# Trunk of an encoder on one core: copies of K by block, kept convolution buffers, and other due times for decays, sweeps and first loads

## The chip, the core and the metric

The kernel runs on one core of one Trainium2 chip. The metric is the device time of one execution in microseconds (us). Of the kernel before, three runs gave a median of 2223.15 us (2220.03 to 2225.03).

The core's engines work side by side, each through its own queue in order: TensorE (PE, with its weight loads as PEld), VectorE (DVE), ScalarE (ACT), GpSimd (POOL) and SyncE (SP), which here only issues transfers. They wait for each other by semaphores.

## The reference, cut to what matters

Two groups of tokens (1024 and 256, together T = 1280, width 1024) go through two layers with shared weights and a last RMS norm. All is float32.

```python
# layer 0
proj = h @ w_in; q, k, v, g = split(proj, 4)          # 16 heads of 64
s = where(mask, (q * 64 ** -0.5) @ k.T + bias, -1e30) # windows of 8 x 16 tokens
h = x + (softmax(s) @ v * silu(g)) @ w_out
# layer 1
proj = rmsnorm(h) @ w_in                              # q, k: 8 heads of 128, v: 8 of 256, z, beta, a
qkv = silu(depthwise_conv5(proj[..., :4096], conv_w))
g = -exp(a_log) * softplus(a + dt_bias); beta = sigmoid(b)
q, k = l2norm(q) * 128 ** -0.5, l2norm(k)
o = chunked_delta(q, k, v, g, beta) + flipped(chunked_delta(flipped inputs))
h = h + (rmsnorm(o, norm_w) * silu(z)) @ w_out
```

The chunked form inverts, for each chunk of the tokens, a unit triangular matrix made of `k k^T`, beta and the decays `exp(g_i - g_j)`; then a scan over the chunks carries a state of 128 x 256 per head and direction.

## The kernel before, in words

**How order is made.** The program is traced once in Python. Long products are traced step by step, and after each matmul `side.tick(columns)` counts its columns. Side work (one attention head, one convolution, one inversion) is a generator; `side.add(chain, delay, pace)` starts it `delay` columns later, and each `yield n` in it asks for its next piece after `n * pace` more columns. So a due time is a place in the traced order, in matmul columns. A planner then orders each engine's instructions by that order and by when it holds them ready in its own model: what is ready early may move ahead. `tc.keep_in_program_order(ins)` binds an instruction behind all that was traced before it on its engine. A tile of a pool with one buffer can be taken again once the last reader of the one before has ended; a closed pool's memory is taken again in the same way.

**Layer 0.** `qk_head(h)` projects q and k of a head in three blocks of tokens (512, 512, 256), splits them into high and low parts (Q, KH, KL), and copies KH and KL from partitions 64 to 127 to partitions 0 to 63 by two transfers of all columns, behind the last block (lines 199 to 201); head 15 copies each block by itself (lines 195 to 197). `g_pair(p)` makes the gates of two heads. `attention(h)` is side work: scores S (lines 286, 287), softmax, transposes, products with V. Before the loop over heads stands `qk_head(0)`, then `g_pair(0)` alone; in the loop attention h runs beside the projections of head h + 1.

**Layer 1, projections.** `gdn_proj` goes through 32 feature blocks of w_qkv in `order` (k of a head ahead of its q and v), each of 30720 columns. A block's product goes to one of two `raw` tiles; `conv(f, r)` then runs as side work: a first tap on ScalarE into `acc`, four taps on VectorE, Silu on ScalarE, a spill to DRAM. With the k of a head, `invert` is added: the squares of k (line 649), scaling (line 657), 30 substitution steps on VectorE (lines 681, 683), called a sweep here, then after a `yield` four rounds of small products (lines 713, 720, 733, 741) with copies between them. `decays` makes the matrix E of decays for a head (product at line 606, adds on VectorE at 609, Exp on ScalarE at 615); of head 1 it is added from the first inversion. `factors` makes per-token factors for the scan from all heads' norms; it is called in the last inversion, behind its sweep. Gate products (`gate_z`) are put between.

**Layer 1, scan.** `prep(h)` loads kT, qT, vT (six pieces, by token block), E (as Al), the decay rows qe and the inverses W of a head, turns and scales them; of head 0 it runs alone beside the last gate product, of the others beside the scan of the head before. `Scan` then takes chunk pairs; its first product is line 1024. `finish` and `Out` make the gated output and the last product.

The pools: `gp` belongs to `gdn_proj` and is closed after it; `prep`, `even` and `odd` hold the scan's inputs; PSUM of the large products (`pmm`) has three buffers.

Of the kernel before, what the change touches and what calls it, by code (L numbers as in the profile page):

```python
# [8 lines left out]
F32 = mybir.dt.float32  # L9
# [3 lines left out]
OP = mybir.AluOpType  # L13
# [3 lines left out]
T = NP + NS  # L17
KD = 8
BLK = [(0, 512), (512, 512), (1024, 256)]
# [16 lines left out]
def layer0(ctx, tc, a, h1_out):  # L36
# [136 lines left out]
    with st:  # L173
# [5 lines left out]
        def qk_head(h, side=None):  # L179
            wh, wl = load_w(tc, a, a["w_qk"][h])  # L180
            Q = ap.tile([128, T], F32R, name="Q", bufs=2)
            KH = ap.tile([128, T], F32R, name="KH", bufs=2)
            KL = ap.tile([128, T], F32R, name="KL", bufs=2)
            for b, (t0, n) in enumerate(BLK):
                ps = pmm.tile([128, 512], F32, name="mm")
                proj(nc, ps[:, :n], wh, wl, XH, XL, b, side)
                c = slice(t0, t0 + n)
                t = ap.tile([128, 512], F32, name="t", bufs=2)
                nc.vector.tensor_mul(t[:, :n], ps[:, :n], rb[:, c])
                nc.scalar.activation(Q[0:64, c], t[0:64, :n], AF.Copy)  # L190
                nc.scalar.activation(KH[64:128, c], t[64:128, :n], AF.Copy, scale=0.125)
                nc.vector.tensor_sub(Q[64:128, c], t[0:64, :n], Q[0:64, c])
                nc.vector.scalar_tensor_tensor(KL[64:128, c], t[64:128, :n], 0.125, KH[64:128, c],
                                               op0=OP.mult, op1=OP.subtract)
                if h == 15:
                    for K in (KH, KL):
                        nc.scalar.dma_start(K[0:64, c].bitcast(F32), K[64:128, c].bitcast(F32))
            if h < 15:
                for K in (KH, KL):
                    nc.scalar.dma_start(K[0:64, :].bitcast(F32), K[64:128, :].bitcast(F32))  # L200
            return Q, KH, KL
# [159 lines left out]
        G, wg = {}, None  # L361
        g_pair(0, G, range(3))
        O = ap.tile([128, T], F32, name="O", bufs=1)
        GS, nV = [G, *({} for p in range(7))], V
        for h in range(16):
# [3 lines left out]
            if h < 14:  # L369
                side.add(attention(h, qkk, V, G, O), 2000, (1.6, 1.5, 1.5, 1.35)[h % 4] if h else 0.75)  # L370
            elif h == 14:
                qks, done[15] = {14: qkk}, 0
                side.add(last_pair(qks, V, G, O), 2000, 0.6)
            side.tick(0)
            q = (h + 1) // 4
            if h % 4 == 0:
# [85 lines left out]
def gdn_proj(tc, a, pmm, XH, XL):  # L462

    nc = tc.nc
    with ExitStack() as st:
# [7 lines left out]
        nc.sync.dma_start(cw, a["conv_w"])  # L473
        raw = [ap.tile([128, T + 6], F32, name=f"raw{i}", bufs=1) for i in range(2)]
        for r in raw:
# [27 lines left out]

        def conv(f, r):

            h, ch = divmod(f, 4)
            m = T + 2
            acc = ap.tile([128, T + 2], F32, name="acc")
            nc.scalar.activation(acc, r[:, 2:2 + m], AF.Copy, scale=cw[:, f, 2:3])  # L509
            yield 8000  # L510
            for i in (0, 1, 3, 4):
                tap = nc.vector.scalar_tensor_tensor(acc, r[:, i:i + m], cw[:, f, i:i + 1], acc,  # L512
                                                     op0=OP.mult, op1=OP.add)
                if i == 0:
                    tc.keep_in_program_order(tap)
            yield 14000 if ch == 1 else 20000
            th = ap.tile([128, T + 2], F32, name="th")
            tc.keep_in_program_order(nc.scalar.activation(th, acc, AF.Silu))
            nc.sync.dma_start(a["qkv_dram"][f, :, :NP], th[:, :NP])
            nc.sync.dma_start(a["qkv_dram"][f, :, NP:], th[:, NP + 2:])  # L520
            if ch == 1:
                side.add(invert(tc, a, ap, pp, h, th, D, W, WT, Z, Bs), 4000, 0.85 if h == 7 else 0.95)
# [3 lines left out]
        for h, ch in order:  # L526
# [4 lines left out]
            for b in sorted(range(3), key=lambda b: (f, b) not in a["begun"]):  # L531
# [7 lines left out]
                nc.scalar.activation(r[:, t0 + o:t0 + o + n], ps, AF.Copy)  # L539
            side.add(conv(f, r), 0)  # L540
            side.tick(0)
            if ch == 1:
                gate_blocks(1 if h in (0, 7) else 2)
        gate_blocks(1)
        side.drain()
# [91 lines left out]
def invert(tc, a, ap, pp, h, kT, D, W, WT, Z, Bs):  # L637
# [22 lines left out]
    if h == 0:  # L660
        a["side"].add(decays(tc, a, ap, pp, 1, Bs), 30000)
    sl = [slice(32 * i, 32 * i + 32) for i in range(4)]
# [45 lines left out]
    elif h:  # L708
        factors(tc, a)
    yield 42000 if h == 0 else 34000  # L710
    zt = pp.tile([128, NB, 32], F32, name="m", bufs=2)
# [46 lines left out]
def gates(tc, a, ap, pmm, pp, XH, XL):  # L758
# [5 lines left out]
    nc.gpsimd.memset(GR.bitcast(F32), 0.0)  # L764
    ab_f = ap.tile([128, T + 2], F32, name="acc")[0:64, :T]
    for b in (0, 2, 1):
# [83 lines left out]
def factors(tc, a):  # L850
# [5 lines left out]
    nc.vector.tensor_scalar(nw, nw, 0.5, None, op0=OP.mult)  # L856
    nc.vector.tensor_scalar(ss, ss, -1.0, None, op0=OP.mult)
    r = cp.tile([128, 8, NB], F32, name="r")
# [18 lines left out]


def prep(tc, a, ap, tp, p_t, h, W, X, alone=False):

# [3 lines left out]
    ident = a["ident"]  # L884
    kT = ap.tile([128, T], F32, name="kT")
    qT = tp.tile([128, T], F32, name="qT")
    nc.sync.dma_start(kT, a["qkv_dram"][4 * h + 1])
    nc.sync.dma_start(qT, a["qkv_dram"][4 * h])
    K = ap.tile([128, NB, 128], F32, name="K")
# [3 lines left out]
    sq = ap.tile([128, NB], F32, name="sq")  # L893
    vT = []

    def rows(*bs):
        for b in bs:
            t0, n = BLK[b]
            for i in range(2):
                t = tp.tile([128, n], F32, name=f"vT{b}{i}")  # L900
                nc.sync.dma_start(t, a["qkv_dram"][4 * h + 2 + i, :, t0:t0 + n])
                vT.append(t)

    if alone:
        rows(0)
    nc.sync.dma_start(AL.bitcast(F32), a["e_dram"][h])
    if alone:
        rows(1, 2)
    for d in range(2):
        nc.sync.dma_start(qe[:, d], a["eg_dram"][8 * d + h].partition_broadcast(128))  # L910
    if not alone:
        rows(0, 1, 2)
    lo, hi = slice(0, 64), slice(64, 128)
# [3 lines left out]
    X[:] = kT, V, K, qe, (AH, AL), W, sq  # L917
    yield 28000 if alone else 6000
    for c0 in range(0, NB, 4):
# [25 lines left out]
        for c1 in range(c0, c0 + n, 2):  # L945
            pv = p_t.tile([128, 2, 256], F32, name="t")
            for c in range(2):
                o = 128 * (c1 - c0 + c)
                for i in range(2):
                    nc.tensor.transpose(pv[:, c, 128 * i:128 * i + 128], vT[c0 // 2 + i][:, o:o + 128], ident)  # L950
                turned = order(nc.scalar.activation(V[:, c1 + c], pv[:, c], AF.Copy,
                                                    scale=a["nk"][:, h, c1 + c:c1 + c + 1]))
# [371 lines left out]
def trunk(ctx, tc, a):  # L1324
# [38 lines left out]
    a["ss"] = a["gc"].tile([128, 8, NB], F32, name="ss")  # L1363
    a["nrk"] = a["gc"].tile([128, 8, NB], F32, name="nrk")
    a["zp"] = left.enter_context(pool(tc, "zp", 2))
    gdn_proj(tc, a, pmm, XH, XL)
# [6 lines left out]
    side = Side()  # L1373
    side.add(prep(tc, a, ap[0], tp, p_0, 0, W[0], X[0], True), 0, 0.5)
    side.tick(0)
# [138 lines left out]
```

## Time and profile before

| What | Value |
|---|---|
| Profiled execution | 2223.32 us |
| its span, first to last instruction | 2221.5 us |
| Median of 3 runs | 2223.15 us |
| PE busy | 2151.7 us, 97% of the span |
| DVE, ACT, POOL busy | 1508.1, 1153.9, 582.8 us |
| Mean granted clock of TensorE | 0.986 |

The span is one execution, taken by the hardware profiler. "Busy" is the time in which at least one instruction of an engine runs. The granted clock is the share of TensorE's full clock; its two levels here are 0.50 (1.2 GHz) and 1.00 (2.4 GHz), and the number of a stretch is the mean. A row of waits names the engine that waited and its line, then the engine, tile and line whose end let it go; "issue" is a wait that the profile can't put down to an instruction. L713 is line 713 of the kernel before.

### The profile page before, as it was taken

How to read it: one execution, taken by the hardware profiler on the slowest of the kernel's cores; microseconds unless marked ns; L12 is line 12 of the kernel's file. 1: busy time of each engine (PE TensorE's matmuls, PEld its weight loads, DVE VectorE, ACT ScalarE, POOL GpSimd, SP SyncE). 2: the span in 40 equal slices, each digit the busy share in tenths (PEclk: the TensorE clock that was granted, in tenths of full speed). 3: DMA queues.
4: the chain of work that ended last, by engine and by line, in shares of the span. 5: the costliest groups of instructions: out<-in, count | busy, mean ns of one | idle time of the engine just before them, and what ended most of it. 6: DMA issues, size and time to landing. Idle time of an engine off the chain costs nothing. (4 is left out here: it accounts for less than half of the span.)

```text
span 2221.5 us, 34043 instructions
## 1 busy us (share of the span) xinstructions
PE 2151.7 (97%) x12502; PEld 1871.1 (84%) x12502; DVE 1508.1 (68%) x3370; ACT 1153.9 (52%) x2319; POOL 582.8 (26%) x631
## 2 busy tenths in 40 slices
PE   8999999999999999999999999999899999999998
PEld 7789989889878877888888888888788888877887
DVE  6577777677672759768687776886566666675444
ACT  6455554555572555363545546454466666654323
POOL 2101110110140332332232313321276666600000
PEclk9999999999999999899999999999899999999999
DMA  5534343542557344344535445352765656566322
GB/s 183 113 76 108 94 117 77 121 100 75 132 162 207 102 112 114 108 120 126 156 106 148 124 139 141 103 155 65 258 157 170 181 180 194 153 212 223 108 97 86
DMA packets 148456, 300.10 MB, mean 135 GB/s; under 512 B 44976, under 2 KB 67632, under 8 KB 147264
## 3 DMA queue, kind: packets, MB, share of 16 engines
q1 hardware_dynamic: 126784, 232.89, 33.3%
q0 software_dynamic: 12096, 44.05, 11.2%
q10 hardware_dynamic: 9408, 20.98, 3.1%
q8 instruction: 99, 1.62, 0.3%
q14 instruction: 69, 0.57, 0.1%
HBM read 211.92 MB, written 75.45 MB: 129 GB/s over the span
## 5 line engine op out<-in xcount | busy, mean ns | idle before, releaser
L1260 PE MATMUL mm<-xh,wh 128*128 128x512 f32 (+1 forms) x1920 | 697.5, 363 | 4.2 <-DVE z L554 1.8
L1260 PE MATMUL mm<-xh,wl 128*128 128x512 f32 (+1 forms) x1920 | 697.8, 363 | 3.0 <-DMA wl<-w_o 2.3
L1260 PE MATMUL mm<-xl,wh 128*128 128x512 f32 (+1 forms) x1920 | 699.8, 364 | 0.3 <-DVE xl L352 0.2
L1260 PEld LDWEIGHTS mm<-xh,wh 128*128 128x128 f32 x1920 | 366.0, 191 | 49.1 <-DVE z L554 2.4
L1260 PEld LDWEIGHTS mm<-xh,wl 128*128 128x128 f32 x1920 | 366.0, 191 | 45.8 <-DMA wl<-w_o 2.7
L1260 PEld LDWEIGHTS mm<-xl,wh 128*128 128x128 f32 x1920 | 366.2, 191 | 42.3 <-DVE xl L352 0.4
L512 DVE SCALAR_TENSOR_TENSOR acc<-raw,cw,acc 128x1282 f32<-128x1282 f32 x128 | 200.9, 1569 | 44.9 <-ACT acc L509 42.0
L1210 POOL CAST wh<-wraw 128x1024 fp32r<-128x1024 f32 x32 | 34.5, 1078 | 498.2 <-PE mm L1260 442.5
L1212 ACT ACTIVATE wh<-wraw 128x1024 fp32r<-128x1024 f32 x92 | 96.9, 1055 | 129.6 <-PE mm L1260 105.4
L1260 PE MATMUL mm<-yh,wh 128*128 128x512 f32 (+1 forms) x384 | 137.4, 359 | 2.0 <-ACT yh L1134 1.9
L1260 PE MATMUL mm<-yh,wl 128*128 128x512 f32 (+1 forms) x384 | 137.0, 358 | 1.2 <-DVE wl L1214 1.2
L1260 PE MATMUL mm<-yl,wh 128*128 128x512 f32 (+1 forms) x384 | 137.6, 359 | 0.3 <-DVE yl L1135 0.3
L1028 DVE TENSOR_TENSOR vl<-k,vh 128x256 fp32r<-128x256 f32 x160 | 67.0, 423 | 69.5 <-ACT vh L1027 65.0
L247 ACT ACTIVATE ph<-pt 128x512 fp32r<-128x512 f32 (+2 forms) x144 | 67.4, 478 | 75.9 <-PE pt L243 65.1
L248 DVE TENSOR_TENSOR pl<-pt,ph 128x512 fp32r<-128x512 f32 (+2 forms) x144 | 75.1, 538 | 39.3 <-ACT ph L247 38.0
L539 ACT ACTIVATE raw<-mm 128x512 f32<-128x512 f32 (+1 forms) x96 | 49.7, 520 | 94.4 <-PE mm L1260 92.8
L1216 ACT ACTIVATE wl<-wraw 128x1024 fp32r<-128x1024 f32 x84 | 88.6, 1055 | 15.7 <-DMA wraw<-w_qk 7.7
L221 ACT ACTIVATE P<-P,mx 128x384 f32<-128x384 f32 (+1 forms) x128 | 75.0, 587 | 39.3 <-DVE mx L220 38.0
L1027 ACT ACTIVATE vh<-k 128x256 fp32r<-128x256 f32 x160 | 60.4, 379 | 62.5 <-PE k L1024 59.2
L1276 PE MATMUL mm<-wh,xl 128*128 128x256 f32 x320 | 91.9, 287 | 0.6 <-POOL xl L65 0.6
L1276 PE MATMUL mm<-wl,xh 128*128 128x256 f32 x320 | 91.5, 286 | 0.5 <-DVE wl L1214 0.5
L1276 PE MATMUL mm<-wh,xh 128*128 128x256 f32 x320 | 91.7, 288 | 0.1
(314 smaller groups left out, 4862.3 us busy)
## 6 DMA issues: line engine op xcount, KB each, us to landing
wraw<-w_qkv SPq DMA_DIRECT2D x32, 512.0 KB, 3.8
qkv_spill<-th SPq DMA_DIRECT2D x32, 512.0 KB, 2.7
wraw<-w_go SPq DMA_DIRECT2D x32, 512.0 KB, 3.6
wl<-w_qkv POOLq DMA_DIRECT2D x30, 512.0 KB, 7.7
Al<-e_spill SPq DMA_DIRECT2D x8, 1280.0 KB, 7.5
qe<-eg_spill SPq DMA_DIRECT2D x16, 640.0 KB, 7.6
wraw<-w_qk SPq DMA_DIRECT2D x16, 512.0 KB, 3.9
wl<-w_qk POOLq DMA_DIRECT2D x16, 512.0 KB, 8.6
```

The lines of the kernel that those rows point to most:

```text
L221: nc.scalar.activation(Pv, Pv, AF.Exp, scale=-1.0, bias=mx[:, 0:1], accum_out=mx[:, 1:2])
L247: nc.scalar.activation(view(ph), view(pt), AF.Copy)
L248: nc.vector.tensor_sub(view(pl), view(pt), view(ph))
L512: tap = nc.vector.scalar_tensor_tensor(acc, r[:, i:i + m], cw[:, f, i:i + 1], acc, op0=OP.mult, op1=OP.add)
L539: nc.scalar.activation(r[:, t0 + o:t0 + o + n], ps, AF.Copy)
L1027: nc.scalar.activation(vh, pw, AF.Copy)
L1028: nc.vector.tensor_sub(vl, pw, vh)
L1210: nc.gpsimd.tensor_copy(wh, raw)
L1212: nc.scalar.activation(wh, raw, AF.Copy)
L1216: nc.scalar.activation(wl, raw, AF.Copy, scale=-1.0)
L1260: nc.tensor.matmul(ps, w[:, k, :], x[k][b], start=(k == 0 and i == 0), stop=(k == KD - 1 and i == 2))
L1276: nc.tensor.matmul(ps, x[k][b][:, cc], w[:, k % 4, :], start=(k == 0 and i == 0), stop=(k == KD - 1 and i == 2))
```

## The change

Eight edits, cut to their core:

- heads 0 and 1 copy KH and KL by block, as head 15 does;
- the gates of pair 0 are traced behind the adding of attention 0, with side work between their matmuls; attention 0 has pace 1.6 in place of 0.75;
- the two `raw` and the two `acc` tiles of the convolutions move from `gp` to a new pool `ep`, which stays open to the end of the scan; the scan's qT, both vT and the kT of even heads take these tiles, so vT is two whole tiles in place of six pieces;
- the last convolution waits 2000 and 14000 columns in place of 8000 and 20000;
- `first_in` loads kT, qT and vT of head 0, 18000 columns after the last convolution is added;
- prep of head 0 starts after 5000 columns at pace 1, before 28000 at pace 0.5;
- the decays of head 1 start after 6000 columns in place of 30000; line 713 is due 46000 (head 0) and 44000 (head 7) columns after the sweep, before 42000 and 34000;
- the first instruction of `factors` that touches the norms is kept in program order, and what needs it follows.

```diff
@@ -192,10 +192,10 @@
                                                op0=OP.mult, op1=OP.subtract)
-                if h == 15:
+                if h in (0, 1, 15):
                     for K in (KH, KL):
                         nc.scalar.dma_start(K[0:64, c].bitcast(F32), K[64:128, c].bitcast(F32))
-            if h < 15:
+            if h not in (0, 1, 15):
                 for K in (KH, KL):
@@ -359,7 +359,6 @@
         G, wg = {}, None
-        g_pair(0, G, range(3))
         O = ap.tile([128, T], F32, name="O", bufs=1)
@@ -367,11 +366,13 @@
             if h < 14:
-                side.add(attention(h, qkk, V, G, O), 2000, (1.6, 1.5, 1.5, 1.35)[h % 4] if h else 0.75)
+                side.add(attention(h, qkk, V, G, O), 2000, (1.6, 1.5, 1.5, 1.35)[h % 4])
             elif h == 14:
...
             side.tick(0)
+            if h == 0:
+                g_pair(0, G, range(3), side)
             q = (h + 1) // 4
@@ -471,7 +472,7 @@
         nc.sync.dma_start(cw, a["conv_w"])
-        raw = [ap.tile([128, T + 6], F32, name=f"raw{i}", bufs=1) for i in range(2)]
+        raw = [a["ep"].tile([128, T + 6], F32, name=f"raw{i}") for i in range(2)]
         for r in raw:
@@ -501,19 +502,21 @@
 
-        def conv(f, r):
+        def conv(f, place):
 
...
             m = T + 2
-            acc = ap.tile([128, T + 2], F32, name="acc")
+            r = raw[place]
+            last = f == 31
+            acc = a["ep"].tile([128, T + 6], F32, name=f"acc{place}")[:, :T + 2]
             nc.scalar.activation(acc, r[:, 2:2 + m], AF.Copy, scale=cw[:, f, 2:3])
-            yield 8000
+            yield 2000 if last else 8000
             for i in (0, 1, 3, 4):
...
                     tc.keep_in_program_order(tap)
-            yield 14000 if ch == 1 else 20000
+            yield 14000 if ch == 1 or last else 20000
             th = ap.tile([128, T + 2], F32, name="th")
@@ -537,10 +540,11 @@
                 nc.scalar.activation(r[:, t0 + o:t0 + o + n], ps, AF.Copy)
-            side.add(conv(f, r), 0)
+            side.add(conv(f, (n_c - 1) % 2), 0)
             side.tick(0)
...
                 gate_blocks(1 if h in (0, 7) else 2)
+        side.add(first_in(tc, a), 18000)
         gate_blocks(1)
@@ -658,7 +662,7 @@
     if h == 0:
-        a["side"].add(decays(tc, a, ap, pp, 1, Bs), 30000)
+        a["side"].add(decays(tc, a, ap, pp, 1, Bs), 6000)
     sl = [slice(32 * i, 32 * i + 32) for i in range(4)]
@@ -707,7 +711,7 @@
         factors(tc, a)
-    yield 42000 if h == 0 else 34000
+    yield {0: 46000, 7: 44000}.get(h, 34000)
     zt = pp.tile([128, NB, 32], F32, name="m", bufs=2)
@@ -762,7 +766,7 @@
     nc.gpsimd.memset(GR.bitcast(F32), 0.0)
-    ab_f = ap.tile([128, T + 2], F32, name="acc")[0:64, :T]
+    ab_f = a["ep"].tile([128, T + 6], F32, name="acc1")[0:64, :T]
     for b in (0, 2, 1):
@@ -854,7 +858,7 @@
     nc.vector.tensor_scalar(nw, nw, 0.5, None, op0=OP.mult)
-    nc.vector.tensor_scalar(ss, ss, -1.0, None, op0=OP.mult)
+    tc.keep_in_program_order(nc.vector.tensor_scalar(ss, ss, -1.0, None, op0=OP.mult))
     r = cp.tile([128, 8, NB], F32, name="r")
@@ -876,46 +880,52 @@
 
+def at(a, name):
+    return a["ep"].tile([128, T + 6], F32, name=name)[:, :T]
+
+
+def first_in(tc, a):
+
+    nc = tc.nc
+    a["first_in"] = at(a, "acc0"), at(a, "acc1")
+    a["vT"] = [at(a, "raw0"), at(a, "raw1")]
+    for i, t in ((1, a["first_in"][0]), (0, a["first_in"][1]), (2, a["vT"][0]), (3, a["vT"][1])):
+        nc.sync.dma_start(t, a["qkv_dram"][i])
+    yield 0
+
+
 def prep(tc, a, ap, tp, p_t, h, W, X, alone=False):
...
     ident = a["ident"]
-    kT = ap.tile([128, T], F32, name="kT")
-    qT = tp.tile([128, T], F32, name="qT")
-    nc.sync.dma_start(kT, a["qkv_dram"][4 * h + 1])
-    nc.sync.dma_start(qT, a["qkv_dram"][4 * h])
+    if alone:
+        kT, qT = a["first_in"]
+    else:
+        kT = ap.tile([128, T], F32, name="kT") if h % 2 else at(a, "acc0")
+        qT = at(a, "acc1")
+        nc.sync.dma_start(kT, a["qkv_dram"][4 * h + 1])
+        nc.sync.dma_start(qT, a["qkv_dram"][4 * h])
+    vT = a["vT"]
     K = ap.tile([128, NB, 128], F32, name="K")
...
     sq = ap.tile([128, NB], F32, name="sq")
-    vT = []
-
-    def rows(*bs):
-        for b in bs:
-            t0, n = BLK[b]
-            for i in range(2):
-                t = tp.tile([128, n], F32, name=f"vT{b}{i}")
-                nc.sync.dma_start(t, a["qkv_dram"][4 * h + 2 + i, :, t0:t0 + n])
-                vT.append(t)
-
-    if alone:
-        rows(0)
     nc.sync.dma_start(AL.bitcast(F32), a["e_dram"][h])
-    if alone:
-        rows(1, 2)
     for d in range(2):
...
     if not alone:
-        rows(0, 1, 2)
+        for t0, n in BLK:
+            for i in range(2):
+                nc.sync.dma_start(vT[i][:, t0:t0 + n], a["qkv_dram"][4 * h + 2 + i, :, t0:t0 + n])
     lo, hi = slice(0, 64), slice(64, 128)
...
     X[:] = kT, V, K, qe, (AH, AL), W, sq
-    yield 28000 if alone else 6000
+    yield 5000 if alone else 6000
     for c0 in range(0, NB, 4):
@@ -945,9 +955,9 @@
             for c in range(2):
-                o = 128 * (c1 - c0 + c)
+                o = 128 * (c1 + c)
                 for i in range(2):
-                    nc.tensor.transpose(pv[:, c, 128 * i:128 * i + 128], vT[c0 // 2 + i][:, o:o + 128], ident)
+                    nc.tensor.transpose(pv[:, c, 128 * i:128 * i + 128], vT[i][:, o:o + 128], ident)
                 turned = order(nc.scalar.activation(V[:, c1 + c], pv[:, c], AF.Copy,
@@ -1362,6 +1372,7 @@
     a["nrk"] = a["gc"].tile([128, 8, NB], F32, name="nrk")
+    a["ep"], a["first_in"] = even.enter_context(pool(tc, "ep", 1, "right")), None
     a["zp"] = left.enter_context(pool(tc, "zp", 2))
@@ -1371,7 +1382,7 @@
     side = Side()
-    side.add(prep(tc, a, ap[0], tp, p_0, 0, W[0], X[0], True), 0, 0.5)
+    side.add(prep(tc, a, ap[0], tp, p_0, 0, W[0], X[0], True), 0, 1)
     side.tick(0)
```

## Rows read from the trace of the kernel before

**Rows 1.** The page, busy time of each engine, share of the span and instructions.

```profile
PE 2151.7 (97%) x12502; PEld 1871.1 (84%) x12502; DVE 1508.1 (68%) x3370; ACT 1153.9 (52%) x2319; POOL 582.8 (26%) x631
```

**Rows 2.** Stage table: stretch, busy us (count) by engine, granted clock, DMA.

```profile
795.00:935.00 140.00, 127.40 (x662) 108.71 (x663) 105.85 (x248) 74.85 (x110) 38.97 (x32) 0.93 0.41 115
...
935.00:1480.00 545.00, 544.19 (x3082) 476.79 (x3082) 412.53 (x870) 283.67 (x409) 149.61 (x147) 1.00 0.48 132
...
1520.00:1600.00 80.00, 66.80 (x365) 57.23 (x364) 36.87 (x49) 36.14 (x67) 16.70 (x27) 0.86 0.51 162
```

**Rows 3.** Waits of PE, 60 to 135 us: total us, times, longest.

```profile
PE S L286 <- DMA KH<-KH: 4.2, 1, 4.2
```

**Rows 4.** Stage table of the stretches behind the waits, with the granted clock.

```profile
109.70:116.50 6.80, 5.89 (x17) 5.06 (x18) 2.87 (x7) 2.07 (x5) 0.00 (x0) 0.50 0.13 28
891.40:898.10 6.70, 6.70 (x35) 6.70 (x33) 3.52 (x6) 4.99 (x8) 4.15 (x5) 0.50 0.00 0
901.60:911.80 10.20, 7.54 (x27) 6.81 (x28) 6.22 (x7) 3.86 (x6) 2.25 (x3) 0.50 0.54 140
1526.30:1536.40 10.10, 9.91 (x33) 8.73 (x34) 0.00 (x0) 7.84 (x11) 1.58 (x3) 0.50 0.64 183
1587.70:1601.20 13.50, 7.69 (x29) 5.92 (x28) 7.51 (x16) 8.01 (x19) 4.74 (x8) 0.50 0.46 148
```

**Rows 5.** Waits of PE, 795 to 935 us.

```profile
PE m L733 <- POOL B L631: 2.8, 1, 2.8
...
PE m L713 <- ACT X L696: 1.8, 1, 1.8
...
PE t L606 <- DVE E L609: 1.7, 1, 1.7
```

**Rows 6.** Waits of PE, 1480 to 1600 us.

```profile
PE m L713 <- issue: 4.4, 1, 4.4
...
PE t L950 <- ACT V L951: 3.4, 3, 2.6
...
PE t L937 <- ACT q L934: 3.2, 1, 3.2
```

**Rows 7.** Timeline, 55 to 130 us: start, us, engine, line, op, tiles, form.

```profile
55.85 0.69 DVE L193 SCALAR_TENSOR_TENSOR KL<-t,KH 64x512 fp32r<-64x512 f32 x1
...
61.86 0.40 PE L1260 MATMUL mm<-xh,wh 128*128 128x512 f32 x1
...
62.09 0.40 PE L1260 MATMUL mm<-xl,wh 128*128 128x512 f32 x1
```

**Rows 8.** Copies of K: whole, heads 0 and 1 (L200); then by block (L197).

```profile
DMA to landing us min/median/max: 8.4/8.8/9.0
...
L197 ACTq DMA_DIRECT2D KH<-KH x3: 468/468/469, 619.6 to 636.4; - x3
...
DMA to landing us min/median/max: 1.9/3.6/4.0
```

**Rows 9.** Groups of DVE, 836 to 901 us: busy us, mean ns, idle before.

```profile
L609 DVE SCALAR_TENSOR_TENSOR E<-t,lbG,mask 128x128 f32<-128x128 f32 x20 | 5.6, 341 | 0.0
```

**Rows 10.** Groups of DVE, 1481 to 1518 us: the factors, two of nine.

```profile
L846 DVE SCALAR_TENSOR_TENSOR rt<-rt,ss 128x80 f32<-128x80 f32 x4 | 1.0, 241 | 0.0
...
L843 DVE TENSOR_SCALAR r<-r 128x80 int32<-128x80 int32 x1 | 0.2, 189 | 0.0
```

**Rows 11.** Timeline of DVE at L722; the wait in PE's weight queue at L713.

```profile
1540.62 0.51 DVE L722 STREAM_TRANSPOSE WT<-m 32x320 f32<-32x320 f32 x1 [17.24 <-PE m L720]
...
L713 PEldq EVENT_SEMAPHORE  x1: 8587/8587/8587, 1517.8 to 1517.8; - x1
```

**Rows 12.** SyncE at kT; then L925 of PE, first and last start.

```profile
1564.85 0.41 SPq L887 DMA_DIRECT2D kT<-qkv_spill  x1
...
L925 PE MATMUL t<-qT,kT x20: 271/275/275, 1572.5 to 1584.0; 128*128 128x128 f32 x20
```

**Rows 13.** Loads of vT in the scan, 1640 to 1930 us.

```profile
L901 SPq DMA_DIRECT2D vT<-qkv_spill x32: 319/352/1275, 1641.3 to 1883.0; - x32
```

## The prediction

> **What bounds the kernel now.** I read the page first, then the stage table, the waits of PE in each stage, the clock of the stretches after those waits, and last the lines behind each wait. The page puts PE at 97% of the span [rows 1]: only PE's work, its waits and its clock can set the end. In the stage table the reader is to compare two kinds of stretch. From 935 to 1480 us PE is busy 544.2 of 545 us at full clock: nothing is to be had there. From 795 to 935 it loses 12.6 us and from 1520 to 1600 13.2 us, at mean granted clocks of 0.93 and 0.86 [rows 2]. A third loss, near 106 us, is one wait of 4.2 us [rows 3]. Behind these waits the granted clock stands at 0.50, the level of 1.2 GHz, for a stretch each [rows 4]. Work done there would take half the time at 2.4 GHz, so a stretch costs half of PE's busy time in it, as long as PE sets the pace. Four places can pay:
>
> A, first head: 4.2 + 5.89/2 = 7.1 us. C, first sweep (around 880 to 912): waits of 2.8 + 1.8 + 1.7 = 6.3 [rows 5], clock (6.70 + 7.54)/2 = 7.1, together 13.4. D, last sweep: 4.4 [rows 6] + 9.91/2 = 9.4. E, end of the projections: 3.4 + 3.2 = 6.6 [rows 6] + 7.69/2 = 10.4. That is 40.3 us, the ceiling of what I can name.
>
> To turn columns into time: a 512-column matmul follows the one before it after 0.23 us [rows 7], so 1000 columns are 0.44 us.
>
> **A: copies of K by block, gates after the first attention is queued.** The first S of head 1 waits for its K copied to the other partitions. Two copies of 320 KB were issued after the last block; such copies took 8.4 to 9.0 us from issue to landing [rows 8]. Now six copies go out, two after each block. The first S of a head reads only block 0, whose copies leave two blocks sooner (24 matmuls of 512 columns and 24 of 256, 8 us); that exceeds the wait of 4.2, so it goes. Where the program already splits these copies, one took 1.9 to 4.0 us, median 3.6 [rows 8]. The four more issues in each of heads 0 and 1 (the first now with them) cost ScalarE's queue 0.47 us each, 3.8 us in all [rows 8]; ScalarE is busy 52% of the span [rows 1], and PE sees them only if a softmax stands right behind.
> The Trainium skill (DMA: Bandwidth & Descriptors, "Anatomy of one DMA — SWDGE (gpsimd) path") gives a transfer a fixed cost of about 2 us and little for its bytes, a rule against splitting; it is fitted on the GpSimd path, and these copies go by ScalarE's queue. By its figures three pieces are an estimated 6.9 us and one whole copy 2.8, and A would gain nothing from the split. The trace disagrees: 8.8 for a whole copy, 3.6 for a piece.
> Attention 0 now starts beside the gate products of pair 0, not after them. Its first S comes 2000 columns after the end of the head's projections, near 61.9 + 0.9 = 62.8 us; block 0 of its K is complete at 56.5 [rows 7]. With a 4.0 us copy it has landed; with 9.0 us it lands at 65.5 and PE waits 2.7 us, and a half-clock stretch like the first of rows 4 costs 2.9 more. So A lies between 7.1 and 1.5. I take 7, by the split copies, the nearest row.
>
> **C: second decays at 6000 columns in place of 30000, L713 due after 46000 in place of 42000.** The edit adds no work: the same 20 adds of VectorE, 5.6 us [rows 9], and their exponentials. 24000 columns are 10.5 us: the last four adds (1.4 us) move ahead of the sweep's end, and the wait of L606 for an add (1.7) meets a VectorE that is less far behind. L713 comes 4000 x 0.95 = 3800 columns, 1.7 us, later in PE's order, about what it waits (1.8), less what moved ahead of it. The 2.8 us of L733 hang on VectorE too: the row names a POOL addition, but the other operand, WT, comes from VectorE's transposes, which queue behind convolution taps. VectorE has its own backlog here, and the edit only moves work. Bounds: all 13.4 on one side; on the other a sweep that ends later by all 20 adds, and one more half-clock stretch like the second of rows 4 (3.4): -9. I take 5: two waits (3.5) and a fifth of the clock.
>
> **D: factors behind the last sweep, 44000 in place of 34000.** Before, the nine groups of the factors (18 instructions, 5.3 us in all) stand between the steps of the last sweep on VectorE [rows 10]. Pinned, they run behind it, into a stretch where VectorE sat idle for 17.2 us until L722 [rows 11]: hidden, unless L722 comes 12 us sooner. The sweep ends 5.3 us earlier, and PE reaches L713 10000 x 0.85 = 8500 columns (3.8 us) later. PE's queue stood at L713 for 8.6 us before it could go, 4.4 of them with nothing left to do [rows 6, 11]; 9.1 us of room cover both. Late next is L722's chain, with some 60000 columns (26 us) of projections beside it. Bounds: 0, if the moved L713 meets another backlog, and 9.4; I take 9.
>
> **E: earlier loads for head 0.** Before, kT was issued at 1564.9 us and the first product of prep ran at 1572.5 [rows 12], well into the last gate product; PE then ran out of projections and waited for ScalarE's part. Now the last convolution is traced over 16000 columns in place of 28000 (5.3 us sooner), its buffers live in a pool that stays, and kT, qT and both vT are loaded when these come free, ahead of the last gate product. Prep starts 5000 columns into that product (before 28000 x 0.5 = 14000): 4.0 us sooner, at half the density. Al, qe and W still wait for the released pool; the products with Al hold VectorE, and behind them stand the gate's sums, but three blocks have three PSUM buffers. Bounds: 0 (Al, qe and W land no sooner and the end stays) and 10.4. I take 7, two thirds: the start is 9 us sooner against 6.6 of waits, but ScalarE's chain is as long as it was.
>
> **Sum.** 7 + 5 + 9 + 7 = 28 us off the profiled execution of 2223.3 (its span 2221.5 and 1.8 around it); the median of the runs, 2223.15, is the same to 0.2. Forecast: **2195 us**; its own range, from half of the sum to the ceiling, 2183 to 2209.
>
> **Rivals.**
> 1. VectorE bounds the first sweep, and the decays brought forward push its end: C is -9 in place of +5, 2209 us. For it: VectorE is busy 105.9 of 140 us there [rows 2], and idle in it mostly for PE. Against: the later heads run the same chain with 34000 and PE loses nothing [rows 2].
> 2. E gives nothing: SyncE holds the first loads until the last Silu, and Al, qe and W decide. For it: these loads need buffers that the last Silu frees. 2223 - 7 - 5 - 9 = 2202 us.
> 3. The planner, not the due times, sets the order on each engine; of the edits only the pin and the split copies hold, and new waits with their half-clock stretches (3 to 7 us each) take most of their 16 us back: 2220 us, no change.
> 4. Slower: the scan. Both vT become one kept tile each in place of six pieces. Before, the pieces' loads go out as each piece is freed, a head ahead, 32 from 1641 to 1883 us in the stretch shown [rows 13]. Should loads into a kept tile stay at the place of their own prep, behind kT, Al, qe and W, each of seven heads waits for up to a landing, 9 us by the longest copy of rows 8; at 6 us a head 42 us more, 2237. It decides from 28/7 = 4 us a head. Against: nothing in the code binds these loads to that place, and they wait only for the turns that read the same columns.
>
> **How the numbers follow.** Forecast 0.54, rival 1 0.12, rival 2 0.13, rival 3 0.09, rival 4 0.09, and 0.03 for more than the ceiling. A measurement of this kernel tells 0.2% (4.4 us) from no change. Faster: forecast, rivals 1 and 2 and the 0.03, less 0.02 for several failing together: 0.80; same 0.10; slower 0.10. Range: from 2180 (the ceiling, and 3 us at a place I did not name) to 2219, which leaves out rival 4 and half of rival 3.
>
> **What would show it.** A: no wait of L286 for a DMA near 106, no half clock behind it. C: L713 and L733 without their waits, a half-clock stretch fewer around 890 to 912. D: the factors behind L688 on VectorE, no wait at L713 near 1520. E: kT issued before the last gate product starts, the first scan product closer to the last projection, no half clock. I am wrong if PE's idle time between 60 and 1600 us falls by less than 10 us, or if the scan (340 us from 1600) grows.

## The result, and the profile after

The changed kernel takes 2198.42 us (median of 4 runs, 2195.85 to 2202.99), the kernel before beside it 2221.59 (4 runs); ratio 0.9898, 95% interval 0.9881 to 0.9915. Measured again later, with the experiments, it took 2201.22 (0.9907, 0.9892 to 0.9923). That is 21 to 23 us less; 28 were forecast. The profiled execution took 2197.81 us, its span 2196.0.

From here lines are those of the kernel after: L713, L720, L733, L606, L609 and L1260 of before are now L717, L724, L737, L610, L613 and L1270; L950 is L960.

The page's busy times, as in [rows 1]:

```profile
PE 2145.2 (98%) x12502; PEld 1869.6 (85%) x12502; DVE 1511.3 (69%) x3370; ACT 1148.2 (52%) x2315; POOL 583.6 (27%) x631
```

PE does the same 12502 matmuls in 6.5 us less, as fewer of them ran at half clock (37.5 us of it ahead of PE's last matmul, 51.2 before); the rest of the 25.5 us by which the span is shorter came out of its idle time. The stage table of the kernel after: stretch, its length, busy us (count) of PE, PEld, DVE, ACT and POOL, granted clock, DMA share, GB/s. The first row is the first head, the second the first sweep, the third the untouched middle, the fourth the last sweep and the end of the projections:

```profile
61.00:147.00 86.00, 85.58 (x497) 74.50 (x495) 62.46 (x168) 46.42 (x106) 9.11 (x10) 1.00 0.45 106
...
795.00:925.00 130.00, 121.67 (x656) 104.86 (x655) 111.13 (x260) 65.75 (x99) 40.49 (x32) 0.96 0.49 134
925.00:1465.00 540.00, 540.00 (x3065) 473.63 (x3064) 407.15 (x855) 282.29 (x409) 151.37 (x147) 1.00 0.48 132
...
1500.00:1580.00 80.00, 71.95 (x397) 62.17 (x395) 40.87 (x63) 39.01 (x73) 16.85 (x29) 0.89 0.59 184
```

The first head has 0.4 us of idle time and no half clock left. The first sweep still loses 8.3 us of PE (12.6 before [rows 2]). The last row loses 8.1 at a clock of 0.89. The waits of PE in these two stretches (us in total, times, longest) answer [rows 5] and [rows 6]:

```profile
PE m L717 <- ACT X L700: 2.7, 1, 2.7
PE t L610 <- DVE E L613: 2.4, 2, 1.3
PE t L653 <- DVE E L613: 1.7, 1, 1.7
...
PE m L717 <- issue: 4.4, 1, 4.4
PE t L960 <- ACT V L961: 2.1, 1, 2.1
PE u L1006 <- ACT vh L1037: 1.2, 1, 1.2
```

The 2.8 us of the third product group are gone, those of the first grew from 1.8 to 2.7. The 4.4 us of the last sweep stand there unchanged, to the tenth. All stretches at half clock but the kernel's tail, from the stage table:

```profile
666.38:669.79 3.41, 3.41 (x10) 2.65 (x9) 0.42 (x1) 3.41 (x5) 0.86 (x1) 0.50 1.00 381
...
782.43:789.25 6.82, 6.82 (x16) 4.03 (x16) 1.32 (x4) 1.76 (x5) 0.00 (x0) 0.50 0.00 0
...
881.42:891.66 10.24, 10.11 (x48) 10.14 (x48) 10.10 (x7) 6.41 (x10) 10.03 (x7) 0.50 0.17 66
...
1509.47:1519.71 10.24, 10.11 (x34) 8.88 (x35) 3.11 (x2) 7.56 (x11) 1.53 (x3) 0.50 0.64 181
...
1570.91:1577.73 6.82, 5.66 (x20) 4.53 (x20) 2.46 (x7) 4.36 (x10) 3.04 (x6) 0.50 0.95 330
```

The first two stand where the kernel before had none: ahead of the first PE waits 3.05 us for w_o, the weights of layer 0's output product; before it waited 2.31.

For E, SyncE's loads ahead of the scan (count, ns, first and last start), and the first products of prep on PE (L935, L925 of before):

```profile
L893 SPq DMA_DIRECT2D raw<-qkv_spill x2: 319/320/320, 1529.4 to 1536.6; - x2
L893 SPq DMA_DIRECT2D acc<-qkv_spill x2: 751/1019/1287, 1531.8 to 1538.9; - x2
...
L935 PE MATMUL t<-acc,acc x20: 270/275/276, 1548.4 to 1565.0; 128*128 128x128 f32 x20
```

All four loads (kT is the first of the two into acc, at 1531.8) are issued 26 to 35 us before that of kT in [rows 12], and the first product stands 24 us earlier, while the program as a whole is 17 us ahead there.

### The profile page after: what moved, and what is told of

Read it like the earlier page. It is cut to its first block, busy times and chain, and to the rows that moved or that the text cites. A ratio compares the mean times of both kernels' runs of the same rounds, so it can differ in the third digit from the quotient of the medians.

```text
span 2196.0 us, 34059 instructions
## 1 busy us (share of the span) xinstructions
PE 2145.2 (98%) x12502; PEld 1869.6 (85%) x12502; DVE 1511.3 (69%) x3370; ACT 1148.2 (52%) x2315; POOL 583.6 (27%) x631
## 4 chain that ended last, share of the span: by engine, by line
PE 84%; DVE 6%; DMA 3%; ACT 3%; issue 2%; POOL 1%; SPq 0%; ACTq 0%; DVEq 0%; POOLq 0%
PE mm L1270 53%; PE mm L1286 4%; PE k L1034 3%; PE o L1006 3%; PE k L1025 2%; PE O L263 2%; PE u L1006 2%; PE o L1047 2%; PE pt L243 2%; DVE acc L515 1%; DMA yt<-y_spill 1%; PE S L287 1%; PE t L960 1%; PE m L1116 1%; PE S L286 1%
## 5 line engine op out<-in xcount | busy, mean ns | idle before, releaser
L1270 PE MATMUL mm<-xh,wl 128*128 128x512 f32 (+1 forms) x1920 | 699.4, 364 | 3.0 <-DMA wl<-w_o 3.0
L1270 PE MATMUL mm<-xl,wh 128*128 128x512 f32 (+1 forms) x1920 | 701.3, 365 | 0.3 <-DVE xl L352 0.2
L1270 PE MATMUL mm<-xh,wh 128*128 128x512 f32 (+1 forms) x1920 | 698.9, 364 | 2.7 <-ACT raw L542 0.9
L1270 PEld LDWEIGHTS mm<-xh,wh 128*128 128x128 f32 x1920 | 365.9, 191 | 46.8 <-ACT raw L542 1.5
L1270 PEld LDWEIGHTS mm<-xh,wl 128*128 128x128 f32 x1920 | 365.8, 191 | 45.2 <-DMA wl<-w_o 3.5
L1270 PEld LDWEIGHTS mm<-xl,wh 128*128 128x128 f32 x1920 | 366.0, 191 | 41.7 <-DVE xl L352 0.4
L1270 PE MATMUL mm<-yh,wh 128*128 128x512 f32 (+1 forms) x384 | 137.8, 360 | 1.4 <-ACT yh L1144 1.3
L1270 PE MATMUL mm<-yh,wl 128*128 128x512 f32 (+1 forms) x384 | 137.1, 359 | 1.1 <-DVE wl L1224 1.1
L1270 PE MATMUL mm<-yl,wh 128*128 128x512 f32 (+1 forms) x384 | 137.7, 360 | 0.3 <-DVE yl L1145 0.3
```

The costliest lines, as they stand in the source:

```text
L1270: nc.tensor.matmul(ps, w[:, k, :], x[k][b], start=(k == 0 and i == 0), stop=(k == KD - 1 and i == 2))
```

## The experiments

Every kernel's trace is cut at three points that all have: the first decay product (L606 of before), the middle one of the 20 products of L713 behind the last sweep, and the first projection behind the scan; the last stage ends with PE's last matmul. The table gives the length of the four stages in us, and in brackets how much of it was at half clock; then the median of all runs, and the ratio to the kernel before with its interval. One profiled run stands behind the stages, 4 to 12 runs behind the median. The kernel before was measured anew beside each group of runs, so kernels of different groups are better compared by their ratios than by their medians.

| kernel | to first decay | to last sweep's products | to end of scan | rest | median us, ratio |
|---|---|---|---|---|---|
| before | 810.6 (6.8) | 718.0 (22.9) | 424.9 (21.5) | 257.5 | 2219.35 to 2221.95 |
| after | 801.6 (10.2) | 710.2 (12.5) | 416.8 (14.8) | 257.0 | 2198.42, 0.9898 |
| after_again | 802.0 (3.4) | 710.5 (14.1) | 417.1 (16.6) | 258.2 | 2201.22, 0.9907 (0.9892 to 0.9923) |
| A_only | 808.8 (17.1) | 713.6 (15.2) | 423.2 (15.5) | 256.5 | 2209.76, 0.9957 (0.9941 to 0.9974) |
| copies_only | 801.4 (3.4) | 714.6 (15.5) | 423.8 (18.6) | 256.7 | 2208.81, 0.9955 (0.9939 to 0.9971) |
| gates_only | 814.9 (10.2) | 714.2 (14.7) | 422.5 (19.5) | 257.4 | 2223.13, 1.0016 (1.0004 to 1.0029) |
| C_only | 816.0 (20.5) | 709.1 (10.8) | 424.2 (23.4) | 258.1 | 2218.81, 0.9996 (0.9986 to 1.0005) |
| D_only | 809.0 (3.4) | 713.7 (14.0) | 426.7 (23.5) | 256.8 | 2219.76, 1.001 (0.9999 to 1.0021) |
| E_only | 812.3 (17.1) | 716.4 (18.2) | 417.3 (12.5) | 256.7 | 2215.98, 0.999 (0.9978 to 1.0002) |
| without_E | 802.8 (0.0) | 710.7 (14.3) | 426.3 (26.6) | 256.8 | 2209.12, 0.9943 (0.9928 to 0.9957) |
| without_C | 800.8 (0.0) | 714.8 (12.4) | 417.8 (14.9) | 259.1 | 2202.73, 0.9914 (0.9899 to 0.9929) |
| factors_pinned | 803.3 (6.8) | 711.8 (17.1) | 417.5 (17.0) | 257.4 | 2202.17, 0.991 (0.9897 to 0.9923) |
| room_last | 800.2 (0.0) | 709.9 (10.2) | 411.9 (10.2) | 257.6 | 2192.66, 0.9883 (0.9865 to 0.9902) |
| room_both | 800.2 (0.0) | 711.3 (10.2) | 410.9 (10.2) | 257.2 | 2197.34, 0.9893 (0.9875 to 0.9911) |

Read down a column, by who has which part. Stage 1 with the split copies (nine traces): mean 802.3, half clock 4.5; without them (before, C, D, E; gates_only, which has the other half of A, is left out): 812.0, 12.0. So A is -9.7. Stage 2 with C as changed (six): 710.4; without (seven; room_both has a C of its own): 715.0; C is -4.6. Stage 3 with E and 34000 or 44000 columns (five): 417.3; without E (seven): 424.5; E is -7.2. D, in the same stage, gains nothing: without E it is 426.7 and 426.3 in the two traces with D, 422.5 to 424.9 in the five with neither. The sum is -21.5, and the whole measured -20.7 and -23.2. That the parts add up to the whole is in part built in, as traces of the whole stand in each mean.

**First: each part alone.** The edits are cut to their core.

```diff
 A_only
-                if h == 15:
+                if h in (0, 1, 15):
...
-        g_pair(0, G, range(3))
...
+            if h == 0:
+                g_pair(0, G, range(3), side)
 C_only
-        a["side"].add(decays(tc, a, ap, pp, 1, Bs), 30000)
+        a["side"].add(decays(tc, a, ap, pp, 1, Bs), 6000)
...
-    yield 42000 if h == 0 else 34000
+    yield 46000 if h == 0 else 34000
 D_only
-    yield 42000 if h == 0 else 34000
+    yield {0: 42000, 7: 44000}.get(h, 34000)
...
-    nc.vector.tensor_scalar(ss, ss, -1.0, None, op0=OP.mult)
+    tc.keep_in_program_order(nc.vector.tensor_scalar(ss, ss, -1.0, None, op0=OP.mult))
 E_only
+            yield 2000 if last else 8000
...
+        side.add(first_in(tc, a), 18000)
...
+    yield 5000 if alone else 6000
```

A_only. 

> The kernel before with the first head's edits alone (K copied by block for heads 0 and 1, gates of pair 0 beside attention 0). Theory: between the traces of before and after the program is 12.7 us ahead at 603 us, and 3 to 4 us of this go again between 650 and 800 us, by a longer wait for w_o (3.0 in place of 2.3) and half-clock stretches behind it; so A alone saves 8 to 10 us (2212 to 2214), with that wait and the half clock in its trace too. Rival: the stretches at 666 and 782 us come from another part; then A alone saves 12 to 13 (2209) and its trace has none of them.

9.6 less, the theory's number, but not by its reason. The w_o wait is 3.3 us in this trace, with 13.7 us of half clock from it to the first decay; but the trace of C_only shows the same (3.0 and 13.7) and has nothing of A, so that loss is no price of A. It comes and goes from one execution to the next: of the two traces of the changed kernel one has half clock at 782 us and one has not.

C_only. 

> The kernel before with the first sweep's edits alone (second decays at 6000 columns, first sweep's products due after 46000). Theory: 7 to 8 us less (2214 to 2216), as the traces drift apart by 7.7 us between 824 and 1509 us; the 2.8 us wait of the third product group gone, one half-clock stretch fewer. Rival: the drift there comes from the earlier arrival or the kept convolution buffers; then C alone is within 3 us of before.

In its own stage the wait and the half clock go as the theory says, and the stage is 8.9 us shorter than in the trace of before (5.9 than the mean without C). By the runs the rival has it: they are 0.5 us less, with an interval that ends 3.1 below before and so short of the stage's 4.6. Of the 8.9 us the profiled run had lost 5.4 in stage 1, ahead of anything that C touches.

D_only. 

> The kernel before with the last sweep's edits alone (44000 in place of 34000 for head 7, the scaling of ss kept in program order). Theory: nothing changes in the order of PE and of the factors, so within 2 us of before (2220 to 2224), with the 4.4 us wait and the half clock behind it. Rival: the edits do work and the wait in the changed kernel has another cause; then D alone saves 4 to 9 us (2213 to 2218).

The theory holds: no gain, the wait at L713 is 4.4 us again.

E_only. 

> The kernel before with the end of the projections alone (last convolution earlier, first loads into kept convolution buffers, prep of head 0 after 5000 columns at full pace, one kept tile for each half of v). Theory: 8 to 10 us less (2212 to 2214), all of it between 1500 and 1660 us, the scan as long as before. Rival: half of it came by the other parts' earlier arrival; 3 to 5 us less.

The stage is 7.6 us shorter than in before, the median only 3.4, which is the rival's number; the interval (4.9 us less to 0.4 more) doesn't tell it from no change. The next runs take E out of the whole.

**Second: the whole again, and parts taken out of it.** without_E and without_C turn the hunks above back in the changed kernel. factors_pinned is the changed kernel with

```diff
-    nc.vector.tensor_scalar(nw, nw, 0.5, None, op0=OP.mult)
+    tc.keep_in_program_order(nc.vector.tensor_scalar(nw, nw, 0.5, None, op0=OP.mult))
```

after_again. 

> The changed kernel again, beside the kernel before. The four parts alone gave -9.6, -0.5, +0.4 and -3.4 us by medians, -13 together; the whole gave -22.7 from four runs. Theory 1: the parts add up and those four runs had less half clock than usual (mean granted clock 0.991 in them, 0.987 to 0.989 with single parts); then about 2206 here. Theory 2: the parts help one another; then 2196 to 2199 again.

2201.2: between the two theories and nearer to the second. The sum of the single medians (13) falls short of the whole (21); the sum of the stages (21.5) does not.

without_E. 

> The changed kernel with the end of the projections as before; first head, first sweep and last sweep stay as changed. From last Silu to first scan product the traces of the kernels without E took 129 to 132 us from the wait of the last sweep's first product, those with E 122 to 123: so 7 to 8 us more than the changed kernel. Rival: E alone saved 3.4 by the medians; then 3 to 4 us more.

7.9 us more than the changed kernel beside it, as the theory says; stage 3 is back at 426.3.

without_C. 

> The changed kernel with the first sweep as before (second decays at 30000 columns, first products due after 42000). Theory 1 (parts add): 1 to 4 us more than the changed kernel. Theory 2 (C pays only once the program arrives earlier, or with the kept buffers): 6 to 9 more, with the 2.8 us wait of the third product group back and a half-clock stretch behind it.

1.5 more by the medians, the first theory's number (the intervals overlap), and 4.3 by stage 2. PE's waits from 795 to 925 us in this kernel:

```profile
PE m L737 <- POOL B L635: 2.8, 1, 2.8
PE t L610 <- DVE E L613: 2.7, 2, 2.3
PE m L717 <- ACT X L700: 1.9, 1, 1.9
```

The 2.8 us of the third product group are back; with the smaller ones PE waits 13.3 us here and 8.4 in the changed kernel.

factors_pinned. 

> The changed kernel with one more instruction kept in program order: the scaling of nw, which stands ahead of that of ss in the factors. In the changed kernel the kept ss scaling is held only to the instruction traced before it, that scaling of nw, which itself floats ahead. Theory: now the factors stand behind the last sweep on VectorE, the sweep ends 4 to 5 us sooner, the 4.4 us wait of its first product and the half clock behind it go: 4 to 9 us less than the changed kernel. Rival: the wait is PE's own (the trace names only issue) and stays: no change.

No change, though the pin holds now. The theory falls; the rival's number came true, but its reason, a wait of PE's own, falls too, as the rows further down show. VectorE inside the sweep of the changed kernel (start, us):

```profile
1469.32 0.21 DVE L685 TENSOR_TENSOR tmp<-N,X 128x30 f32<-128x30 f32 x1
1469.45 0.19 DVE L868 TENSOR_SCALAR nrk<-nrk 128x80 f32<-128x80 f32 x1
1469.57 0.22 DVE L687 TENSOR_TENSOR X<-X,tmp 128x30 f32<-128x30 f32 x1
1469.69 0.24 DVE L849 TENSOR_TENSOR rt<-r 128x80 f32<-128x80 f32 x1
1469.84 0.22 DVE L685 TENSOR_TENSOR tmp<-N,X 128x58 f32<-128x58 f32 x1
```

and with the factors pinned behind it:

```profile
1474.17 0.20 DVE L685 TENSOR_TENSOR tmp<-N,X 128x30 f32<-128x30 f32 x1
1474.40 0.22 DVE L687 TENSOR_TENSOR X<-X,tmp 128x30 f32<-128x30 f32 x1
1474.66 0.22 DVE L685 TENSOR_TENSOR tmp<-N,X 128x58 f32<-128x58 f32 x1
...
1510.88 0.19 DVE L861 TENSOR_SCALAR ss<-ss 128x80 f32<-128x80 f32 x1
```

From one L685 to the next is 0.52 us with two factors in between and 0.49 without. A step that needs the last one's result starts only when that has ended; an independent instruction starts 0.07 to 0.10 before the end, and fits beside. The sweep runs from the first L670 to the end of L692, first in the changed kernel, then with the factors pinned:

```profile
1462.83 0.49 DVE L670 STREAM_TRANSPOSE D<-B 32x320 f32<-32x320 f32 x1
...
1504.58 1.91 DVE L692 STREAM_TRANSPOSE D<-X 128x1024 f32<-128x1024 f32 x1
```

```profile
1467.53 0.49 DVE L670 STREAM_TRANSPOSE D<-B 32x320 f32<-32x320 f32 x1
...
1508.95 1.94 DVE L692 STREAM_TRANSPOSE D<-X 128x1024 f32<-128x1024 f32 x1
```

That is 43.66 us with all 19 factors and 43.36 with 16 of them gone (the other three, L868 and L870, don't need ss and still float). By their durations the factors in the sweep fell from 5.2 to 1.6 us.

What PE waits for at L717 is behind the sweep. ScalarE in the changed kernel, after the transpose of L692 has ended at 1506.5:

```profile
1506.52 0.47 ACT L700 ACTIVATE X<-D 32x320 f32<-32x320 f32 x1 [4.16 <-DVE D L692]
1506.90 0.45 ACT L701 ACTIVATE X<-D 32x320 f32<-32x320 f32 x1
...
1509.04 0.47 ACT L700 ACTIVATE X<-N 32x320 f32<-32x320 f32 x1
```

```profile
1509.60 4.45 PE L717 MATMUL m<-X,B 128*128 128x32 f32 x20 [4.42 <-issue]
```

L717 reads the half of X that the four copies of L700 write. The last of them ends at 1509.51, and L717 starts at 1509.60: "issue" in the wait's row hides a dependence on ScalarE.

**Third: a later place, and A in halves.**

```diff
 room_last, from the changed kernel
-    yield {0: 46000, 7: 44000}.get(h, 34000)
+    yield {0: 46000, 7: 60000}.get(h, 34000)
 room_both
+    yield {0: 54000, 7: 60000}.get(h, 34000)
 copies_only, from the kernel before: A without its edits at g_pair and attention
 gates_only, from the kernel before: A with "if h == 15" left as it was
```

room_last. 

> The changed kernel with 60000 columns in place of 44000 behind the last sweep. Its first product now stands 16 projection matmuls (3.7 us) later on PE, spread between them; 34000 and 44000 left it at the same place. Theory: PE reaches it when the sweep and ScalarE's copies behind it are nearly done, so of the 4.4 us wait 0.7 or less is left, and the half-clock stretch behind it goes in most runs: 4 to 8 us less than the changed kernel (2193 to 2197). Rival: the later product groups push the end of the projections, where the first scan loads wait for the released pool; then the gain is lost there and the time is the same within 2 us.

The theory holds. It is 8.5 us under after_again by medians, but the kernel before was 2.6 us faster beside it; by the two ratios it is 5.3 us (their intervals still meet). By stage 3 it is 5.4, and there the two traces with 60000 columns (411.9, 410.9) lie clear of the five with E and fewer (416.8 to 417.8). PE's waits from 1490 to 1600 us, and the stage table around L717:

```profile
PE t L960 <- ACT V L961: 3.1, 1, 3.1
PE u L1006 <- ACT vh L1037: 1.2, 1, 1.2
PE m L717 <- issue: 1.0, 1, 1.0
```

```profile
1507.00:1517.00 10.00, 9.28 (x65) 8.72 (x66) 3.91 (x3) 9.87 (x15) 1.96 (x4) 1.00 0.65 185
```

Of the 4.4 us 1.0 is left, at full clock; L960, late next, waits 3.1 in place of 2.1. By its median this is the fastest kernel of the study.

room_both. 

> As the run before it, and 54000 in place of 46000 behind the first sweep (its first product 21 projection matmuls, 4.8 us, later; the trace of the changed kernel waits 2.7 us there). Theory: the 2.7 us and the half clock behind it go as well: 3 to 7 us less than the run before it. Rival: the second sweep starts later or the third product group waits again as in the kernel before (2.8 us); then no gain over it.

The rival: no gain. The 2.7 us of L717 are gone, and the next group waits instead:

```profile
PE m L724 <- ACT Z L720: 3.7, 1, 3.7
```

copies_only. 

> The kernel before with K copied by block in heads 0 and 1, gates of pair 0 where they were. Theory: the copies carry the first head's gain, since the 4.2 us wait of head 1's first S is for them: 6 to 8 us less than before, no wait there and no half clock behind it. Rival: the early gates carry it; 0 to 3 less.

10.5 less, more than the theory's 6 to 8: the copies alone carry all of A. The twelve split copies (issue to landing):

```profile
DMA to landing us min/median/max: 1.9/2.4/7.0
```

gates_only. 

> The kernel before with attention 0 queued ahead of the gates of pair 0, K of heads 0 and 1 copied whole. Theory: the first S of head 0 now waits for a whole copy (landing about 9 us after the last block), as head 1's first S still does: within 3 us of before. Rival: PE has gate products to do meanwhile, and the small softmax waits between 99 and 131 us (2 us) go: 2 to 4 less; or, if the early start carries the gain, 6 to 8 less.

3.8 more (0.9 to 6.4 by the interval), just outside the theory's 3: now two S wait for whole copies, until 70.5 and 115.4 us, each with 3.4 us of half clock at its end:

```profile
PE S L286 <- DMA KH<-KH: 8.3, 2, 4.5
```

## Why the prediction was right, and where it was wrong

The whole was right in direction and nearly in size: 2195 forecast, 2198 and 2201 measured. PE's idle time between 60 and 1600 us fell from 41.1 to 25.1 us, and the scan did not grow, so by its own signs it stands. That the sum came so near is in part luck: one of the four terms gave nothing, another came by waits that it had not counted, and A gave 2.7 us more than was put down for it. By its terms:

- **A, 7 forecast, 9.7 in the traces.** Right in mechanism. Waits give 6.2: the 4.2 of L286, and 2.0 of softmax waits at 99 to 131 us that I did not name. The other 3.5 is about half of the 7.5 us by which the half clock differs between the two sets of traces; some 3 of it stand behind the wait of L286, the rest is the scatter at w_o. The early gates, which I costed with the copies, give nothing, and without the copies they cost 3.8. A split copy took a median of 2.4 us, a whole one 8.8 [rows 8]. Of the figures of the Trainium skill that I had weighed against the split (DMA: Bandwidth & Descriptors, "Anatomy of one DMA — SWDGE (gpsimd) path"), which are fitted on the GpSimd path, the estimate for a piece of 128 KB, 2.3 us, is near what these copies took, and the 2.8 for a whole one is not; three pieces come to 6.8 by them, not 6.9.
- **C, 5 forecast, 4.6 in the traces.** The size came out by luck, not by the mechanism. The sum took 3.5 us for the waits of L606 and L713 and left out the 2.8 of L733. With C the first two did not go: L610 waits 2.4 us and L717 2.7, where they were 1.7 and 1.8. What went is L737's (2.8 and 1.0), and PE's waits there are 4.9 us less in all than in without_C. The clock's share came as forecast: half of the 2.9 us by which the mean half clock of stage 2 differs is 1.5, and a fifth of 7.1 was taken. The timed runs give 0.5 and 1.5 for C and can't confirm the 4.6; and which of its two edits carries it no run shows.
- **D, 9 forecast, 0. This step failed**, in all its three parts. "Pinned, they run behind it": the factors stand in the sweep of after as in [rows 10]. So keep_in_program_order does not bind an instruction behind all that was traced before it, as I had put it. What fits is that it holds ss only to the scaling of nw, traced just before, which itself floats ahead: with nw pinned too, ss runs behind the sweep. "The sweep ends 5.3 us earlier": I added up durations (of 18 instructions; the groups have 19); with the pin mended it is 0.3 us shorter. "PE reaches L713 10000 x 0.85 = 8500 columns (3.8 us) later": 234 projection matmuls stand between the last norms and L713 in both kernels, so that due time did not set the place; 60000 did, 16 matmuls later. That the planner's own estimate of the sweep's end set it below that is what fits; the traces don't show that estimate. The term's bound of 0 had another case in mind, a moved L713 that "meets another backlog"; here it did not move. Placed late enough, it gives 5.4 (stage) or 5.3 (ratios) of the 9.
- **E, 7 forecast, 7.2 in the traces**, 7.9 where it is taken out. Right in size, and by the traces in mechanism: the loads went out 26 to 35 us earlier, prep's first product came 7 us earlier than the program as a whole, and of the 6.6 us of waits that were named 2.4 are left (L960 2.1, L947 0.3). Whether the earlier loads, the earlier last convolution or the earlier start of prep carries it no run shows, as E was only moved whole. E alone gave 3.4 by the median.

Rival 1 falls with stage 2, rival 2 with without_E. The ground for rival 1, that VectorE was idle there mostly for PE, was read too high: 16.3 of 32.0 us of its waits from 795 to 935 us were for PE, 10.2 for a transfer. Rival 3 was true of D alone. Rival 4 falls: from its first product to its last the scan takes 389.5 to 391.3 us in the seven traces with E and 387.8 to 392.3 in the seven without, and the timeline of the changed kernel is 25 us ahead at both of its ends.

Not settled: why C and E alone gain less in their timed runs than in their stages (0.5 against 4.6, 3.4 against 7.2). Stages rest on one execution each. Half clock ahead of either edit comes and goes between traces of the same code (stage 1 without A: 3.4 to 20.5 us). The mean granted clock of the timed runs points the same way. In C's twelve it is 0.9874, in the 29 of the kernel before beside them 0.9888, which at 2219 us is 3 us more lost, though C's own stage loses less. In E's twelve it is 0.9888 again, though E's own stage has 15.2 us of half clock in the traces in place of 21.2. So both kernels seem to have lost clock elsewhere; that this is the whole of the gap is argued, not shown.

## What to carry to other kernels

Cost an instruction inside a chain of dependent short ones by the distance between the chain's starts, not by its own duration: beside such steps it may be free, and taking it out then gains nothing. Before crediting a due time or an ordering pin, look which operand the waiting instruction really lacks and whether the order on its engine moved at all; here the wait named "issue" was a copy on ScalarE, and only a due time past the present place moved anything. Compare parts by stage in several traces as well as by medians, when clock stretches of untouched code are as large as the part.

## What the runs showed of the hardware

- In the last sweep an independent short instruction on VectorE started 0.07 to 0.10 us before the end of the one ahead, and a dependent one 0.03 to 0.05 us after the end of the one that it needs. Taking 16 independent instructions out from between the chain's steps lowered the busy time of the factors there from 5.2 to 1.6 us, and the sweep by 0.3 us. The Trainium skill (VectorE: DVE Perf Modes, "Rules for kernel authors") advises to minimise the count of chained operations; those taken out here were no links of the chain, and their count cost 0.02 us each. The same page ("The DRAIN you can't avoid") has an operation that is not held start before the one ahead has emptied, and with that the 0.07 to 0.10 us agree.
- A stretch at half clock cost PE about half its length: A_only and copies_only, which do the same matmuls, differ in stage 1 by 7.4 us, and by 13.7 us of half clock.
- The wait for w_o, which no edit touches, took 1.7 to 3.3 us in the 14 traces. Within 1 us of the end of all six waits of 3.0 us and more the granted clock fell for 3.4 or 6.8 us; of the eight shorter ones it did so at two (2.2 in gates_only, 2.4 in E_only) and not at six (2.3 in the kernel before). In after it fell once more at 782 us, for 6.8 us, with no wait of PE since 666.
